# Attention logits made once, with queries on partitions, and weight halves transposed by DMA for the value product

## Chip, core and metric

One core of a Trainium2 chip runs the whole program in one launch. The metric is device time in microseconds; the kernel before took 2256.42 us (median of three runs, 2255.13 to 2261.94).

## What is computed

A decoder block with two parallel branches over 2048 tokens: sparse attention and a state-space recurrence, merged by gates. The change touches the attention branch. An indexer has chosen 256 keys for each query; in this kernel the choice is a mask `msk`, 0 for a chosen key and -2^60 for the others. The rest of the branch, cut from the reference (`k_sel` and `v_sel` are the chosen keys and values; a chosen key behind the query does not count):

```python
qg = qb.reshape(bsz, Q_BLOCK, ATTN_KV_HEADS, ATTN_GROUP, HEAD_DIM)   # 2 groups of 4 heads, 64 wide
s = jnp.einsum('btkgd,btskd->btkgs', qg, k_sel) * attn_scale
s = jnp.where(valid, s, -jnp.inf)
p = jax.nn.softmax(s, axis=-1)
o = jnp.einsum('btkgs,btskd->btkgd', p, v_sel)
o_a = o.reshape(bsz, Q_BLOCK, ATTN_WIDTH) * jax.nn.silu(z_a)
merged = g_a * (o_a @ w_branch_a) + g_b * (o_b @ w_branch_b)
x = x + merged @ w_out                                               # and a last RMSNorm
```

## The kernel before, in words

Every float32 operand of a large matmul is split in two float16 halves, high and low, and products are summed in PSUM from two or three matmuls of halves. The program runs in sections: normalised and transposed input, the state-space branch, the indexer, the selection beside the projections (until about 1410 us), then the attention and the merge, which is the place of the change.

Tokens are worked in 16 query tiles of 128; tile i has i+1 key tiles of 128. Keys stand transposed in `KK`, one high and one low part for each of the two groups (`KHt`, `K2t`), and the values in `Vt`, with a column of ones between high and low half. Three streams are written as Python generators, and `interleave` lays them beside each other at an even pace:

- `att_A(i)` (L1356) loads the queries of a tile, splits them, transposes both halves by DMA (`Q1`), and makes the largest masked logit of each query: one matmul `lq` of 512 columns (L1386) and one masked maximum on VectorE (L1389) for each head and 512 keys, queries on partitions. The negated maximum goes beside the queries into a second tile `q2t`, which another DMA transposes (`Q2`, L1404), so that the logits matmul subtracts it.
- `att_B(i)` (L1470) makes the logits a second time, now with keys on partitions and 4 heads x 128 queries as columns (L1483, L1485), adds the transposed mask `mkt` (L1492, loaded by a DMA transpose at L1353), takes the exponential (L1493), rounds it to float16 (`ph`, L1497) and subtracts for the low half (`pl`, L1500, GpSimd). Keys are already on the partitions, so `pv` (L1419) and `pv_lo` (L1428) use `ph` and `pl` as stationary sides as they are. `LAG` = 3 such steps lie between making a weight and using it. The column of ones gives the softmax sum. `tail` multiplies by the gate and splits and transposes the tile's output (`oT`).
- `fin_M` and `fin_O` (L1505 to L1577) are merge and output projection of earlier tiles: per tile 72 and 48 matmuls of 512 columns, with DMA loads `obt`, `gtl`, `xr` and a DMA transpose of the merged tile (`mT`). They fill PE between the attention's matmuls.

The generators give an emission order; the framework's scheduler then sets the order on each engine, and every DMA is issued from the one SP queue, in its order. Buffers come in rings (`bufs`), and an instruction waits until the ring's oldest user is done.

## Time and profile before

| | |
|---|---|
| runs | 2255.13, 2256.42, 2261.94 us |
| profiled execution | span 2252.5 us; no time of its own is listed, the median of the runs lies 3.9 us above the span |
| TensorE matmuls (PE) | 2045.4 us busy, 91% of the span |
| VectorE (DVE) | 1832.5 us, 81% |
| ScalarE (ACT) | 1129.4 us, 50% |
| GpSimd (POOL) | 840.0 us, 37% |
| DMA, one hardware queue | 226 MB, 37.8% of 16 engines |
| mean granted TensorE clock | 0.966 |

Busy time is the union of an engine's rows. A matmul's row lasts from its start to its modelled end and overlaps the next one, so a count of starts says more than busy time. "Granted clock" is the share of full speed that TensorE was given. An engine's idle time before an instruction is put down to the instruction or DMA that released it.

### The profile page before, as it was taken

The page shows a single profiled execution, that of the slowest core. Times are in us where ns is not written, and L with a number is a line of the kernel's source. Part 1 is how long each engine was busy: PE and PEld are TensorE (multiplying, and loading weights), DVE is VectorE, ACT ScalarE, POOL GpSimd, SP SyncE. Part 2 cuts the span into 40 slices and gives each one's busy share as a digit, 9 for nine tenths or more (in the row PEclk, how much of TensorE's full clock was granted, in tenths as well). Part 3 has the DMA queues.
Part 4 walks back from the last instruction along what each step waited for, and adds up shares of the span by engine and source line. Part 5 has one row for each costly group of instructions (what it writes and reads, how often), then busy time and mean ns, then how long its engine had stood idle before and what let it go on. Part 6 is the DMA issues. An engine that isn't in the chain of part 4 may idle for free. (4 is left out here: it accounts for less than half of the span.)

```text
span 2252.5 us, 43654 instructions
## 1 busy us (share of the span) xinstructions
PE 2045.4 (91%) x15537; PEld 1391.0 (62%) x15537; DVE 1832.5 (81%) x5156; ACT 1129.4 (50%) x1971; POOL 840.0 (37%) x1208
## 2 busy tenths in 40 slices
PE   6898998899998999899999987988988889999997
...
DVE  8888888988887588888988775577989888888864
...
GB/s 151 121 109 106 104 61 88 103 73 64 64 69 81 109 83 97 116 109 95 120 131 145 78 167 94 120 205 119 108 116 102 100 90 109 67 95 104 66 80 49
DMA packets 371196, 229.07 MB, mean 102 GB/s; under 512 B 209996, under 2 KB 333720, under 8 KB 370968
## 3 DMA queue, kind: packets, MB, share of 16 engines
q1 hardware_dynamic: 370968, 226.19, 37.8%
...
q14 instruction: 104, 0.85, 0.1%
...
## 5 line engine op out<-in xcount | busy, mean ns | idle before, releaser
L1500 POOL TENSOR_TENSOR pl<-p,ph 128x512 f16<-128x512 f32 x272 | 328.3, 1210 | 426.1 <-ACT ph L1497 407.5
L1493 ACT ACTIVATE p<-p,lnb,qsc 128x512 f32<-128x512 f32 x270 | 217.6, 811 | 213.0 <-DVE p L1492 212.8
L428 PEld LDWEIGHTS <-xh 128*128 128x128 f16 x2560 | 252.4, 100 | 46.6 <-ACT kvt L1178 10.3
L429 PEld LDWEIGHTS <-xh 128*128 128x128 f16 x2560 | 250.9, 99 | 47.4 <-issue 12.4
L430 PEld LDWEIGHTS <-xl 128*128 128x128 f16 x2560 | 250.9, 99 | 31.8 <-issue 1.9
L1492 DVE TENSOR_TENSOR p<-lg,mkt 128x512 f32<-128x512 f32 x266 | 181.5, 685 | 55.6 <-PE lg L1485 50.5
L1389 DVE CUSTOM_DVE_ANT_0 jk<-lq,mka 128x512 bf16<-128x512 f32 (+3 forms) x304 | 187.8, 618 | 24.8 <-PE lq L1386 18.7
L1497 ACT CAST ph<-p 128x512 f16<-128x512 f32 x272 | 165.8, 614 | 6.4
L1073 ACT ACTIVATE jkS<-sca,XX 128x384 int8<-128x384 f32 (+3 forms) x104 | 138.6, 1333 | 46.5 <-DVE XX L1063 30.3
L1419 PE MATMUL po<-Vt,ph 128*128 128x129 f16 x1088 | 114.6, 223 | 11.0 <-DVE oa L1442 4.1
L1386 PE MATMUL lq<-KK,Q 128*128 128x512 f16 (+3 forms) x320 | 102.6, 349 | 22.8 <-DVE mxs L1389 16.9
L1485 PE MATMUL lg<-Q,KK 128*128 128x512 f16 x272 | 103.7, 385 | 13.9 <-DMA Q<-q2t 13.9
L1075 DVE TENSOR_SCALAR_CACHE_REDUCE jkV<-sca,XX 128x1536 uint8<-128x1536 f32 (+4 forms) x78 | 111.8, 1434 | 2.4
L1562 PE MATMUL fi<-wo,mT 128*128 128x512 f16 x256 | 98.5, 385 | 10.9 <-DVE gtl L1538 5.1
L1483 PE MATMUL lg<-Q,KK 128*128 128x512 f16 x272 | 104.5, 385 | 2.8 <-DVE p L1492 2.8
L1531 PE MATMUL fi<-wpb,obt 128*128 128x512 f16 x256 | 99.2, 387 | 6.6 <-DVE gtl L1538 4.5
L937 ACT ACTIVATE r<-acc 128x512 f32<-128x512 f32 (+3 forms) x152 | 79.8, 541 | 46.4 <-DVE sca L938 28.8
L1428 PEld LDWEIGHTS <-pl 128*128 128x128 f16 x1088 | 66.3, 99 | 58.7 <-POOL pl L1500 6.1
L1419 PEld LDWEIGHTS <-ph 128*128 128x128 f16 x1088 | 72.3, 99 | 43.5 <-issue 10.8
L1532 PE MATMUL fi<-wpb,obt 128*128 128x512 f16 x256 | 99.0, 387 | 0.0
L1533 PE MATMUL fi<-wpb,obt 128*128 128x512 f16 x256 | 98.7, 386 | 0.0
L1563 PE MATMUL fi<-wo,mT 128*128 128x512 f16 x256 | 98.7, 386 | 0.0
(811 smaller groups left out, 6469.9 us busy)
## 6 DMA issues: line engine op xcount, KB each, us to landing
...
e<-ecr SPq DMA_DIRECT2D x128, 64.0 KB, 3.1
...
```

Source lines behind the costliest of these rows:

```text
L428: PE.matmul(ps, xh[:, c, tk], hi[:, c], start=(first and c == 0), stop=False)
L429: PE.matmul(ps, xh[:, c, tk], lo[:, c], start=False, stop=False)
L430: PE.matmul(ps, xl[:, c, tk], hi[:, c], start=False, stop=(last and c == KC - 1))
L1073: A.activation(jkA[:, :n], sct[i], AF.Sign, bias=thr[:, 0, k:k + 1], scale=-1.0, accum_out=cnt[:, 0, k:k + 1])
L1075: V.tensor_scalar(jkV[:, :n], sct[i], thr[:, 0, k:k + 1], 0.0, OP.is_lt, OP.add, accum_out=cnt[:, 0, k:k + 1])
L1389: V.tensor_tensor_reduce(jk[:, :c1 - c0], ps[:, :c1 - c0], mk[:, c0:c1], 1.0, -BIG, OP.add, OP.max, mxs_[:, h, c:c + 1])
L1419: PE.matmul(B["po"][h // 2][:, h % 2, 0:129], ph[:, h], Vt[:, j, g, 0:129], start=(j == 0 and h % 2 == 0), stop=False)
L1483: PE.matmul(ps, KHt[g][:, js], Q1[:, hs], start=True, stop=False)
L1492: V.tensor_tensor(p32, ps, mb, OP.add)
L1493: A.activation(p32, p32 if masked and not onP else ps, AF.Exp, bias=lnb, scale=qsc[g])
L1497: A.copy(ph, p32)
L1500: PL.tensor_tensor(pl, p32, ph, OP.subtract)
```

## The change

The logits are made once, with queries on partitions. `prep_q` loads and transposes a tile's queries. `weights_h` works one head: for each 512 keys two matmuls (high and low keys) and one masked-maximum instruction that also writes the masked logits to `xm`, carrying the running maximum from chunk to chunk; then one exponential over the whole row, with the maximum as its bias and the softmax sum as an accumulated output. In parts of up to `CH` = 1024 keys the weights are rounded to float16 (`hl`, first part), the remainder subtracted on GpSimd (second part), and both halves transposed by one DMA into `pT`. `values_h` multiplies `pT` by the values, the oldest head first, `LAG` = 2 heads after its weights. The separate maximum pass, `Q2`, the transposed mask and the column of ones are gone. The diff, cut to its core (the removed functions stand above; comments that it removes are left out):

```diff
@@ constants
-PLD = 2
-LAG = 3
-PB = 3
+LAG = 2
+CH = 1024
+XB = 3
+TB = 4
...
-PL_ = 2
-PQ_ = 2
+PL_ = 4
@@ class keys, tile
-            PL.memset(ks[:, :, :, 1, 66:128], 0.0)
-            PL.memset(ks[:, :, :, 1, 64:66], 2.0 ** 15)
...
-            V.tensor_tensor(ks[:, :, :, 1, 0:64], t[:, :, 0:2], ks[:, :, :, 0, 0:64], OP.subtract)
+            for hf in range(2):
+                V.tensor_tensor(ks[:, :, :, 1, hf * 64:hf * 64 + 64], t[:, :, 0:2], ks[:, :, :, 0, 0:64], OP.subtract)
@@ attention: att_A, att_B, pv, pv_lo and load_mt out
...
+    def load_mk(i):
+        mks[i] = at.tile([P, wide if wide < S else S], BF, name="mka")
+        SP.dma_start(mks[i][:, :(i + 1) * P], msk[i, :, :(i + 1) * P])
+    def prep_q(i):
+        q32 = at.tile([P, H, HD], FT, name="q32", bufs=1)
+        SP.dma_start(q32.rearrange("p h d -> p (h d)"), qd[i])
+        yield 1.0
+        while tails:
+            _run_all(tails.pop(0))
+        q1 = at.tile([P, H, 2, HD], F16, name="q1", tag="spa", bufs=1)
+        V.tensor_copy(q1[:, :, 0], q32)
+        V.tensor_tensor(q1[:, :, 1], q32, q1[:, :, 0], OP.subtract)
+        Qs[i] = ac.tile([P, H, P], F16, name="Q1", bufs=2)
+        SP.dma_start_transpose(Qs[i], q1.rearrange("p h a d -> p (h a d)"))
+        yield 2.0
+    def weights_h(i, h, B):
+        n = (i + 1) * P
+        g = h // 4
+        xm = pw.tile([P, wide], FT, name="xm", bufs=XB if wide == S else 2)
+        mxs_ = at.tile([P, 4], FT, name="mxs", bufs=4)
+        c = 0
+        for c0 in range(0, n, 512):
+            c, c1 = c0 // 512, min(n, c0 + 512)
+            ps = lgps2([P, 512])
+            PE.matmul(ps[:, :c1 - c0], Qs[i][:, h], KHt[g][:, c0:c1], start=True, stop=False)
+            PE.matmul(ps[:, :c1 - c0], Qs[i][:, h], K2t[g][:, c0:c1], start=False, stop=True)
+            mk = mks[i][:, c0:c1] if i >= 2 else cmask[:, 2 * P - n:]
+            V.tensor_tensor_reduce(xm[:, c0:c1], ps[:, :c1 - c0], mk, 1.0, mxs_[:, c - 1:c] if c else -BIG, OP.add, OP.max, mxs_[:, c:c + 1])
+            yield (c1 - c0) * 0.85e-3
+        yield None
+        nb = at.tile([P, 1], FT, name="nb", bufs=4)
+        V.tensor_scalar(nb, mxs_[:, c:c + 1], nqsc[g], LNB, OP.mult, OP.add)
+        A.activation(xm[:, :n], xm[:, :n], AF.Exp, bias=nb, scale=qsc[g], accum_out=B["den"][:, h:h + 1])
+        parts = []
+        for k0 in range(0, n, CH):
+            w = min(CH, n - k0)
+            hl = pw.tile([P, 2 * min(CH, wide)], F16, name="hl", bufs=2)
+            A.copy(hl[:, :w], xm[:, k0:k0 + w])
+            PL.tensor_tensor(hl[:, w:2 * w], xm[:, k0:k0 + w], hl[:, :w], OP.subtract)
+            pT = pw.tile([P, 2 * min(CH, wide) // P, P], F16, name="pT", bufs=TB)
+            SP.dma_start_transpose(pT[:, :2 * w // P], hl[:, :2 * w])
+            parts.append((k0 // P, w // P, pT))
+        pend.append((i, h, parts, B))
+    def values_h():
+        i, h, parts, B = pend.pop(0)
+        g, r = h // 4, h % 4
+        if r == 0:
+            B["po"] = psO.tile([P, 4, P], FT, name="po", tag="po")
+        po = B["po"]
+        for j0, nb_, pT in parts:
+            for b in range(nb_):
+                j = j0 + b
+                PE.matmul(po[:, r], pT[:, b], Vt[:, j, g], start=(r == 0 and j == 0), stop=False)
+                PE.matmul(po[:, r, 0:HD], pT[:, nb_ + b], Vt[:, j, g, 0:HD], start=False, stop=(r == 3 and j == i))
+                if b % 4 == 3 or b == nb_ - 1:
+                    yield (b % 4 + 1) * 0.086
+        if r == 3:
+            if g == 0:
+                while tails:
+                    _run_all(tails.pop(0))
+                B["oa"] = at.tile([P, H, HD], FT, name="oa", bufs=1)
+            rc = at.tile([P, 4], FT, name="rc")
+            oag = B["oa"][:, 4 * g:4 * g + 4]
+            V.reciprocal(rc, B["den"][:, 4 * g:4 * g + 4])
+            A.copy(oag, po[:, :, 0:HD])
+            V.tensor_tensor(oag, oag, po[:, :, HD:2 * HD], OP.add)
+            PL.tensor_tensor(oag, oag, rc[:, :, None].to_broadcast([P, 4, HD]), OP.mult)
+            if g == G - 1:
+                tails.append(tail(i, B))
...
+    def att(i):
+        B = {"den": at.tile([P, H], FT, name="den", bufs=2), "za": at.tile([P, H, HD], FT, name="za")}
+        SP.dma_start(B["za"].rearrange("p h d -> p (h d)"), zd[i])
+        n = i + 1
+        for h in range(H):
+            v = values_h() if len(pend) >= (LAG if wide == S else 1) else iter(())
+            ws = weights_h(i, h, B)
+            for w in _zip(iter(lambda: next(ws), None), v, (n + 3) // 4, (n + 3) // 4):
+                if tails and next(tails[0], True) is True:
+                    tails.pop(0)
+                yield w
+            for _ in ws:
+                pass
@@ fin_O
-        sq = fi.tile([P, 512], BF, name="sq", bufs=1)
+        sq = fi.tile([P, 512], I8, name="sq", bufs=1)
@@ pace
-    tA = lambda i: 2.0 + QY + 8 * (i + 1) * P / 2400
-    tB = lambda i: 2.0 * (i + 1)
+    tA = 3.0
+    tB = lambda i: 8 * (i + 1) * (0.85 * 0.128 + 0.086)
```

## The order around the change

Numbers behind a name count buffers. `lq`, `lg`/`lg2` and `fi2` are PSUM tiles, `jk` is scrap.

**DVE, query tile 6 (7 key tiles).** Before, the maxima of this tile (L1389, each with its accumulator read) stand between the masked copies `p32` of the tile before it (L1492):

```order
L1389 ISA jk_19881,mxs_19874<-lq_19879,mka_19749 128x384
L1389 ISA mxs_19874 128x1
L1492 TENSOR_TENSOR p32_19886<-lg2_19883,mkt_19304 128x512
L1389 ISA jk_19906,mxs_19874<-lq_19904,mka_19749 128x512
L1389 ISA mxs_19874 128x1
L1492 TENSOR_TENSOR p32_19919<-lg2_19916,mkt_19304 128x512
L1389 ISA jk_19910,mxs_19874<-lq_19908,mka_19749 128x384
L1389 ISA mxs_19874 128x1
```

Now L1369 writes the masked logits and their maximum at once, two instructions for each of a head's two chunks (512 and 384 keys), and `nb`, the bias of the exponential:

```order
L1374 TENSOR_SCALAR nb_20284<-mxs_20215,nqsc0_9090 128x1
L1369 ISA xm_20292,mxs_20293<-lg2_20294,mka_19707 128x512
L1369 ISA mxs_20293 128x1
L1517 TENSOR_SCALAR s1_19813<-s1_19813 128x1
L1421 TENSOR_TENSOR oa_20041<-oa_20041,za_19710 128x512
L1518 TENSOR_SCALAR s1_19813<-s1_19813 128x1
L1484 SCALAR_TENSOR_TENSOR gtl_20273<-gtl_20273,fi2_20275 128x512
L213 TENSOR_SCALAR fry_20251<-s1_19813 128x1
L1369 ISA xm_20292,mxs_20293<-lg2_20339,mka_19707,mxs_20293 128x384
L1369 ISA mxs_20293 128x1
L214 TENSOR_SCALAR fry_20251<-fry_20251 128x1
```

L1492 is gone from the queue, L1374 came, and the steps of the merge (`gtl`, `s1`, `fry`) stand between as before.

**SP, the DMA queue, at the same place.** Before, in a stretch with the mask loads of tile 7 (8 key tiles) and `Q2` of tile 6:

```order
L1336 DMA_TRANSPOSE mT_19949<-spm_19418 128x16x128
L1378 DMA_TRANSPOSE Q1_20361<-q1_20333 128x8x128
L1577 DMA out_x<-xr_19486 128x512
L1577 DMA out_x<-xr_19487 128x512
L1365 DMA mka_20240<-msk_9063 128x1024
L1353 DMA_TRANSPOSE mkt_20242<-msk_9063 128x8x128
L1554 DMA xr_20145<-in_x 128x512
L1404 DMA_TRANSPOSE Q2_20182<-q2t_9046 128x8x128
L1520 DMA gtl_20758<-gd_9096 128x2x512
L1554 DMA xr_20851<-in_x 128x512
L1361 DMA q32_22013<-qd_9094 128x512
```

Now, around the start of tile 6's heads; `pT` is a head's weights, 14 blocks of 128 columns:

```order
L1319 DMA_TRANSPOSE mT_20180<-spm_19761 128x16x128
L1383 DMA_TRANSPOSE pT_20212<-hl_20209 128x14x128
L1442 DMA za_20625<-zd_9084 128x512
L1383 DMA_TRANSPOSE pT_20290<-hl_20287 128x14x128
L1523 DMA out_x<-xr_19809 128x512
L1523 DMA out_x<-xr_19810 128x512
L1319 DMA_TRANSPOSE oT_20312<-spa_20299 128x8x128
L1383 DMA_TRANSPOSE pT_20359<-hl_20356 128x14x128
L1500 DMA xr_20368<-in_x 128x512
L1500 DMA xr_20904<-in_x 128x512
L1352 DMA_TRANSPOSE Q1_20322<-q1_20319 128x8x128
L1383 DMA_TRANSPOSE pT_20413<-hl_20410 128x14x128
```

The transposes of weights stand between the loads of the merge, and `Q2` and `mkt` are gone.

**PE, logits and value products.** Before, the logits of a step are followed by the value products of an earlier one:

```order
L1485 LDWEIGHTS KK_9097
L1485 MATMUL lg2_20865<-Q2_20658,KK_9097 128x512
L1419 LDWEIGHTS ph_20715
L1419 MATMUL po_20875<-Vt_9098,ph_20715 128x129
L1419 LDWEIGHTS ph_20715
L1419 MATMUL po_20875<-Vt_9098,ph_20715 128x129
L1531 LDWEIGHTS obt_20753
L1531 MATMUL fi2_20847<-wpb0_16607,obt_20753 128x512
```

Now, in tile 6, the last logits of the third head (chunk of 384 keys) and what follows them:

```order
L1366 MATMUL lg2_20339<-KK_9086,Q1_19874 128x384
L1367 LDWEIGHTS Q1_19874
L1367 MATMUL lg2_20339<-KK_9086,Q1_19874 128x384
L1477 LDWEIGHTS obt_20268
L1477 MATMUL fi2_20343<-wpb0_16597,obt_20268 128x512
L1478 LDWEIGHTS obt_20268
L1478 MATMUL fi2_20343<-wpb1_16598,obt_20268 128x512
L1479 LDWEIGHTS obt_20268
```

and the end of the stretch, up to its first value product (`pT_20359` holds its weights):

```order
L1508 LDWEIGHTS mT_20180
L1508 MATMUL fi2_20373<-wo0_18560,mT_20180 128x512
L1509 LDWEIGHTS mT_20180
L1509 MATMUL fi2_20373<-wo1_18561,mT_20180 128x512
L1510 LDWEIGHTS mT_20180
L1510 MATMUL fi2_20373<-wo0_18560,mT_20180 128x512
L1477 LDWEIGHTS obt_20268
L1477 MATMUL fi2_20343<-wpb0_16597,obt_20268 128x512
L1398 LDWEIGHTS pT_20359
L1398 MATMUL po_20324<-Vt_9087,pT_20359 128x128
```

Between the two stand 31 matmuls of merge and output, 8 of logits (the next two heads) and 14 pairs of value products (128 and 64 columns, the two heads before), 22,144 columns together. What was a distance of three steps of 512 columns is now one of one to five heads, which the scheduler set differently from tile to tile.

## Rows read from the trace of the kernel before

**Rows 1.** The page: busy us, share and instructions by engine; busy tenths of two engines.
```profile
PE 2045.4 (91%) x15537; PEld 1391.0 (62%) x15537; DVE 1832.5 (81%) x5156; ACT 1129.4 (50%) x1971; POOL 840.0 (37%) x1208
...
PE   6898998899998999899999987988988889999997
...
DVE  8888888988887588888988775577989888888864
```

**Rows 2.** Stretches of the attention part: length, busy us by engine, clock, DMA share, GB/s.
```profile
core 0: us, PE busy (x) PEld busy (x) DVE busy (x) ACT busy (x) POOL busy (x), PEclk, DMA share, GB/s
1470.00:1520.00 50.00, 41.17 (x231) 19.25 (x229) 37.85 (x113) 20.65 (x34) 14.99 (x16) 0.90 0.77 204
1520.00:1700.00 180.00, 158.64 (x1090) 80.93 (x1089) 155.66 (x465) 105.25 (x174) 82.55 (x81) 0.98 0.50 113
1700.00:1900.00 200.00, 182.50 (x1285) 94.36 (x1285) 176.43 (x490) 119.23 (x191) 92.07 (x87) 0.98 0.38 92
1900.00:2200.00 300.00, 280.87 (x2041) 148.59 (x2040) 247.16 (x634) 196.00 (x312) 151.45 (x137) 0.98 0.36 88
2200.00:2253.00 53.00, 38.81 (x191) 17.10 (x189) 21.02 (x68) 9.66 (x19) 0.80 (x2) 0.92 0.14 47
sum 783.00, PE 701.99 PEld 360.24 DVE 638.12 ACT 450.80 POOL 341.86; mean PE 140.40 PEld 72.05 DVE 127.62 ACT 90.16 POOL 68.37
```

**Rows 3.** Timeline of PE matmuls: start, row length, line, form, count.
```profile
1860.08 0.38 PE L1386 MATMUL lq<-KK,Q 128*128 128x512 f16 x1
1860.30 0.38 PE L1483 MATMUL lg<-Q,KK 128*128 128x512 f16 x1
1860.51 0.38 PE L1485 MATMUL lg<-Q,KK 128*128 128x512 f16 x1
1860.73 0.28 PE L1428 MATMUL po<-Vt,pl 128*128 128x65 f16 x4
1860.85 0.39 PE L1419 MATMUL po<-Vt,ph 128*128 128x129 f16 x4
1861.08 0.38 PE L1562 MATMUL fi<-wo,mT 128*128 128x512 f16 x1
```

**Rows 4.** Waits of PE, 1410 us to the end: total us, times, longest.
```profile
PE lq L1386 <- DVE mxs L1389: 16.9, 29, 1.7
PE lg L1485 <- DMA Q<-q2t: 13.9, 8, 3.2
PE fi L1562 <- DVE gtl L1538: 5.1, 3, 2.5
...
PE fi L1562 <- DMA mT<-spm: 4.6, 3, 2.2
PE fi L1531 <- DVE gtl L1538: 4.5, 3, 2.8
PE po L1419 <- DVE oa L1442: 4.1, 6, 1.4
...
PE lg L1483 <- DVE p L1492: 2.8, 3, 1.1
```

**Rows 5.** Groups by line, 1470 to 2200 us: count, busy us, mean ns, idle before.
```profile
L1500 POOL TENSOR_TENSOR pl<-p,ph 128x512 f16<-128x512 f32 x265 | 320.3, 1211 | 371.6 <-ACT ph L1497 367.6 <-DVE oa L1442 3.2 <-POOL pl L1500 0.2
L1493 ACT ACTIVATE p<-p,lnb,qsc 128x512 f32<-128x512 f32 x264 | 212.9, 811 | 210.9 <-DVE p L1492 210.7
L1492 DVE TENSOR_TENSOR p<-lg,mkt 128x512 f32<-128x512 f32 x263 | 179.5, 685 | 53.9 <-PE lg L1485 48.8 <-POOL pl L1500 3.1 <-PE po L1419 0.6
L1497 ACT CAST ph<-p 128x512 f16<-128x512 f32 x264 | 161.2, 614 | 6.3
L1389 DVE CUSTOM_DVE_ANT_0 jk<-lq,mka 128x512 bf16<-128x512 f32 x224 | 153.3, 684 | 20.4 <-PE lq L1386 16.0
...
L1389 DVE DVE_READ_ACCUMULATOR2_ANT mxs<- 128x1 f32 x296 | 24.2, 82 | 0.0
...
L1330 ACT ACTIVATE spm<-mg,rms 128x1024 f16<-128x1024 f32 x15 | 17.1, 1141 | 0.3 <-DVE rms L1323 0.2
...
L1330 ACT ACTIVATE spa<-oa,ras 128x512 f16<-128x512 f32 x13 | 9.3, 713 | 2.6 <-DVE ras L1323 2.5
...
L1541 ACT ACTIVATION_READ_ACCUMULATOR spm<-mg 128x1 f32 x29 | 5.4, 186 | 0.0
...
L1571 DVE TENSOR_SCALAR s<-s 128x1 f32<-128x1 f32 x14 | 2.9, 205 | 0.1
```

**Rows 6.** DMA transposes, 1470 us to the end: count, median us to landing.
```profile
mT<-spm SPq DMA_TRANSPOSE x15, 4.3
...
Q<-q2t SPq DMA_TRANSPOSE x13, 4.2
oT<-spa SPq DMA_TRANSPOSE x13, 3.1
```

**Rows 7.** Timeline of the SP queue: start, us that the issue takes.
```profile
1596.05 1.25 SPq L1353 DMA_TRANSPOSE mkt<-msk  x1
...
1598.02 1.73 SPq L1404 DMA_TRANSPOSE Q<-q2t  x1
```

More of the change, by code (lines that the diff above doesn't have):

```diff
@@ L874, in hybrid_block @@
     kv = pool("kv", 1, side="right", reuse_waits="tile")
-    lnb = kv.tile([P, 1], FT, name="lnb")
-    V.memset(lnb, 8 * math.log(2.0))
-    q2t = [kv.tile([P, H, P], F16, name="q2t")]
-    for t in q2t:
-        V.memset(t, 0.0)
     kctx = ExitStack()
@@ L1125, in hybrid_block @@
     KHt, K2t = ([KK[:, g, j] for g in range(G)] for j in range(2))
-    Vt = kv.tile([P, NT, G, 130], F16, name="Vt")
-    V.memset(Vt, 1.0)
+    Vt = kv.tile([P, NT, G, 2 * HD], F16, name="Vt")
     nsec = []
@@ L1225, in hybrid_block @@
     qsc = [cst.tile([P, 1], FT, name=f"qsc{k}") for k in range(2)]
+    nqsc = [cst.tile([P, 1], FT, name=f"nqsc{k}") for k in range(2)]
     kvs = keys()
@@ L1372, in att_A @@
         V.tensor_copy(q1[:, :, 0], q32)
         V.tensor_tensor(q1[:, :, 1], q32, q1[:, :, 0], OP.subtract)
-        A.copy(q2[:, :, 0:64], q1[:, :, 0])
-        yield 0.5
-        MARK("attA")
-        Q1 = ac.tile([P, H, P], F16, name="Q1", bufs=2)
-        SP.dma_start_transpose(Q1, q1.rearrange("p h a d -> p (h a d)"))
-        yield QY
-        mxs_ = at.tile([P, H, 4], FT, name="mxs")
-        for h in range(H):
-            for c in range(nck):
-                MARK("attA")
-                c0, c1 = c * 512, min(n, c * 512 + 512)
-                ps = psQ.tile([P, 512], FT, name="lq", tag="lq" if PQ_ else "lg2")
-                PE.matmul(ps[:, :c1 - c0], Q1[:, h], KHt[h // 4][:, c0:c1], start=True, stop=True)
-                jk = pw.tile([P, 512], BF, name="jk", tag="jk", bufs=1)
-                if i >= 2:
-                    V.tensor_tensor_reduce(jk[:, :c1 - c0], ps[:, :c1 - c0], mk[:, c0:c1], 1.0, -BIG, OP.add, OP.max, mxs_[:, h, c:c + 1])
-                else:
-                    if i == 1:
-                        V.tensor_reduce(mxs_[:, h, 1:2], ps[:, 0:P], axis=AX.X, op=OP.max)
-                    V.tensor_tensor_reduce(jk[:, :P], ps[:, n - P:n], cmask, 1.0, -BIG, OP.add, OP.max, mxs_[:, h, 0:1])
-                yield (c1 - c0) / 2400
@@ L1406, in att_A @@
-        yield 0.5
-    pend, plo, tails = [], [], []
-    def pv():
-        MARK("attB")
-        if len(plo) >= (PLD if lag > 1 else 1):
-            pv_lo()
-        i, g, j, ph, pl, B = pend.pop(0)
-        if j == 0:
-            B["po"] = [psO.tile([P, 2, 256], FT, name="po", tag="po") for _ in range(2)]
-        for h in range(4):
-            PE.matmul(B["po"][h // 2][:, h % 2, 0:129], ph[:, h], Vt[:, j, g, 0:129], start=(j == 0 and h % 2 == 0), stop=False)
-        plo.append((i, g, j, pl, B))
-        while j == i and plo:
-            pv_lo()
@@ L1464, in flush @@
         while pend:
[L1465 removed]
+            _run_all(values_h())
         while tails:
             _run_all(tails.pop(0))
[L1469 to L1503 removed]
@@ L1505, in att_B @@
                     tails.pop(0)
-                yield 1.0
+                yield w
+            for _ in ws:
+                pass
     def fin_M(i, fi):
```

139 lines of the change are left out of this document (29 added, 110 removed).

## The prediction, made before any run of the change

> **What bounds the kernel now.** I read the page first [rows 1]: TensorE (PE) is busy 91% of the span and VectorE (DVE) 81%, and both stay at eight or nine tenths in nearly every slice. The change lies in the attention part, so the table of stretches comes next [rows 2]. From 1470 us to the end PE is busy 702 of 783 us, DVE 638; ScalarE (ACT) 451 and GpSimd (POOL) 342 have room, and the DMA engines are at 0.36 to 0.50 after a start at 0.77. A busy matmul row overlaps the next one, so what PE must spend is read from the spacing of starts [rows 3]: matmuls of 512 columns start 0.215 us apart, 0.42 ns a column, four `ph` products of 129 columns take 0.23 us and four `pl` products of 65 take 0.12 us. From its first maximum matmul at 1410 us to the end PE has 1,920 matmuls of merge and output, 544 of logits and 272 of the maximum at 0.215 us, 1,088 pairs of value products at 0.0875, and 23 us of the last projection: 706 of 842 us. So PE is the bound, at 84%. Of the rest, 81 us from 1470 on are idle (the table's sum row), some 23 are half clock (a granted clock of 0.90 to 0.98), the others the latency of matmuls that something waits for. The waits of PE by name [rows 4] are small: 16.9 us for DVE's maxima, 13.9 us for the Q2 transpose, 5.1 and 4.5 us for DVE's merge, 4.1 us for `oa`.
>
> **What goes from PE.** The maximum pass `lq` (L1386) vanishes: for each key tile of each query tile 8 heads x 128 columns. Query tile i has i+1 key tiles, 136 in all, so 272 matmuls of 512 columns x 0.215 = **58 us**. The logits are still two matmuls per 512 columns (queries now the stationary side), and the value products are 128 + 64 columns where they were 129 + 65, so 0.70 us per key tile for 8 heads before and after.
>
> **What goes from DVE, ACT and POOL.** DVE loses the masked copy L1492, 263 x 0.685 = 180 us of its 638 [rows 5], the four small `rm` steps and half of the `oa` blocks, some 40 us; it gains one `nb` step per head, 112 x 0.2 = 22 us. It keeps the reduce with its accumulator read, 0.684 + 0.082 us per 512 columns; that instruction now also delivers what L1492 delivered. DVE falls to some 440 us. On ACT the exponential becomes one instruction per head. By the two lengths of L1330 [rows 5] 512 more columns cost 0.43 us, so a row of n key tiles costs 0.81 + 0.107 (n - 4), and 0.19 for its accumulator; 178 us over tiles 2 to 15 for 213. The copies to half precision cost about 150 for 161, the new `oa` copy 11. POOL's subtraction has the same elements, 1.21 us per 512. None of these three is the bound, before or after, so I count nothing for their totals. What frees PE is that a DVE at 60% keeps it waiting less: of the 33 us that it waits for DVE [rows 4] I take 20 as gone, and with Q2 its 13.9 go wholly: **34 us**. The edits in `keys` (no memsets, one more subtraction), the 8-bit `sq` and the wider `cmask` lie beside matmuls or on engines with room: nothing.
>
> **What comes on the DMA side.** Each head's weights, both halves, are transposed: 2 x 128 columns per key tile and head, 136 x 8 x 256 = 278,528 columns. No transpose of this source stands in the trace, but the same shape does: `mT` (2048 columns, SBUF to SBUF) lands 4.3 us after its issue starts, `oT` (1024) after 3.1 [rows 6], so 1024 columns cost 1.2 us over a fixed 1.9. That makes 326 us of all 16 engines; Q2 and `mkt` (33,000 columns) give back 39. The loop's own DMA time is its shares times its stretches, 320 us [rows 2]; it becomes about 600 of 770, a share near 0.78. The bytes: 1024 columns are 262 KB, in 1.2 us 218 GB/s. The Trainium skill (Advanced Engine Details and Errata, X-Bar Transpose (TRN2)) expects 350 to 400 GB/s; the trace is slower, no transpose in it comes near. By the page's figure the 326 us would be an estimated 190, and the share 0.6.
>
> On the SP queue 192 transposes come and 30 (16 Q2, 14 `mkt`) go. One holds the queue 1.25 to 1.73 us [rows 7], so some 240 us more of issue, in front of the loads of `gtl`, `xr`, `mT` and `oT`, which PE and DVE need. A transpose that waits for POOL also holds all that stands behind it. PE waits for `mT` today 4.6 us in three waits [rows 4]; with twice the DMA load I add 0.5 us for each of 16 tiles: **8 us**. Nothing bounds this from below; from above the Q2 transpose, 4.2 us against the 3.1 of an undisturbed one of its size [rows 6], gives 1.1 us, 18 us in all.
>
> **The new wait.** Before, a step of weights went DVE, ACT, ACT, POOL in 0.69 + 0.81 + 0.61 + 1.21 = 3.3 us and PE came back to it three steps later. Now a head's weights pass a chain after its last logits: reduce 0.77, `nb` 0.2, exponential, copy of up to 1024 columns (1.04), POOL (2.4), transpose (4.3 for 2048 columns), and some 0.5 us for the hand-offs. With the terms above that is 7.7, 8.7, 9.6 and 10.6 us for 5, 6, 7 and 8 key tiles, about 10.5 to 11.5 for more, and the second part of the weights of tiles with 9 and more key tiles lands up to 2.6 us later still. Against it stands PE's own work between a head's last logits and its first value product, counted as columns in the order of the changed program: 7.0, 7.0, 8.4 and 9.1 us on average for 5 to 8 key tiles (the head shown in the order part has 22,144 columns, 9.2 us), 13.7 for 9, 15 to 24 for 10 to 14, 10.1 for 15, and 13.6 for 16. To the chain I add 1 us of queue: undisturbed landings are at the median in `mT` and `oT`, and 1.1 us over it in Q2 [rows 6]. The gaps are then 1.7, 2.7, 2.2 and 2.5 us. Since a stall at one head also holds back the next head's logits, each gap is paid about half: 8 heads x half of 9.1 = 36 us. The last two tiles pay 12 us by their second parts, the first three 8 (their chain is 5 to 7 us, over 4 to 13 of work), and the end, where nothing is left to put between, about 6. Sum **62 us**. Bounds: 39 us with no queue at all, 116 with 3 us; each further us of chain costs about 27.
>
> **Clock.** In the stretch where PE was busy 41 of 50 us the granted clock was 0.90, elsewhere 0.98 [rows 2]. Tiles of 5 to 9 key tiles would now look like that stretch; 0.08 of 180 us is 14, half of it inside waits: **7 us**.
>
> **Sum.** -58 - 34 + 62 + 7 + 8 = -15 us. The profiled execution has a span of 2252.5 us; the median of the runs is 2256.4, 3.9 above it, which I leave as what lies around the span. So 2256 - 15 = **2241 us**, and for this case 2215 to 2262.
>
> **Rivals.**
> *The chain decides (slower).* If a head's weights take 3 us longer than the chain alone, by a blocked SP queue or a DMA queue with other transfers in it, the wait is 116 us instead of 62 and the time 2295; at 4 us 2325. For it: a DMA share near 0.78, in-order SP where `out_x` and `mT` wait for DVE, only two `hl` buffers, so that the copy of a part waits for the transpose two parts back. Against it: the undisturbed landings, and that tiles of 10 to 14 have twice the work between. It turns the sign at about 1.6 us of queue, where the sum is zero.
> *No new wait counts (faster).* PE's order holds enough work, and DVE's relief is real: -58 - 34 = 2164. For it: the slack of tiles 9 to 14; against it: tiles 5 to 8, where the chain is longer than the work even with no queue.
> *The DMA engines bound the loop.* The highest share of a stretch is 0.77. If 600 us cannot be done at more than that, the loop takes 779 of the 783 us it has now, and the time stays at 2252. For it: nothing in the trace runs higher; against it: that stretch was the start, with weights loading.
> That the change does not do what it says can be left out: the order no longer has L1386 or L1492.
>
> **Numbers.** A measurement of this kernel can tell about 0.3% (7 us) from no change. Forecast 0.45 (0.38 of it faster, 0.04 same, 0.03 slower); chain 0.30 (0.02 same, the rest slower); no new wait 0.17, faster; DMA bound 0.08 (0.04 same, 0.04 slower). Faster 0.55, same 0.10, slower 0.35. The range goes from 2165, the full gain, to 2325, the chain with 4 us of queue.
>
> **What would show it.** The new logits line of PE should have 0.215 us starts and no maximum matmuls; DVE near 60% in the loop; the weights' transposes landing at 4.3 to 5.5 us; DMA share about 0.75; PE waiting for `pT` some 60 us, most of it in tiles of 5 to 8 key tiles and hardly any at 10 to 14. Landings of 7 us, or waits for `pT` over 100 us or spread evenly over the tiles, would mean the chain; waits under 20 us the full gain. I am wrong in the mechanism if PE waits mainly for DVE, or if the granted clock falls below 0.9 over most of the loop.

## The result, and the profile after

| | before | after |
|---|---|---|
| median of the runs, us | 2255.99 (2255.13 to 2261.94, 4 runs) | 2340.53 (2334.59 to 2347.95, 4 runs) |
| ratio | | 1.0383, 95% interval 1.036 to 1.0407 |
| profiled execution's span, us | 2252.5 | 2339.4 |

The change is slower by 3.8%, 85 us, where the prediction had it faster by 15; it is also outside the range. The page of the changed kernel, against [rows 1], with the DMA engines' slices below PE's:

```profile
PE 2015.2 (86%) x15313; PEld 1363.9 (58%) x15313; DVE 1678.5 (72%) x4819; ACT 1074.3 (46%) x1891; POOL 807.6 (35%) x1079
...
PE   6799998899999899899998887788878777778877
...
DMA  4443423322223322423453444977886777888981
```

PE has 224 matmuls and 30 us of busy time less; the maximum pass is gone. But its last third stands at seven and eight tenths, where it stood at eight and nine. The stretches, with the columns of [rows 2]:

```profile
1470.00:1520.00 50.00, 35.99 (x177) 16.11 (x176) 23.80 (x73) 19.41 (x46) 12.69 (x13) 0.80 0.98 238
1520.00:1700.00 180.00, 146.47 (x984) 72.15 (x982) 113.48 (x358) 87.42 (x159) 62.68 (x42) 0.97 0.80 170
1700.00:1900.00 200.00, 155.93 (x1065) 77.62 (x1063) 108.07 (x332) 88.93 (x147) 69.19 (x52) 0.97 0.73 156
1900.00:2200.00 300.00, 236.64 (x1728) 120.05 (x1727) 183.83 (x508) 145.69 (x199) 133.70 (x78) 0.96 0.83 171
2200.00:2340.00 140.00, 101.64 (x685) 49.53 (x683) 68.63 (x202) 52.03 (x71) 35.94 (x20) 0.94 0.58 120
sum 870.00, PE 676.67 PEld 335.47 DVE 497.81 ACT 393.49 POOL 314.20; mean PE 135.33 PEld 67.09 DVE 99.56 ACT 78.70 POOL 62.84
```

From 1470 us on PE is now busy 677 of 870 us (702 of 783 before), DVE 498: DVE has room, and PE is less busy all the same. The DMA share is 0.73 to 0.83 from 1520 to 2200 us, where it was 0.36 to 0.50. What PE waits for, and who waits for the weights' chain, from 1410 us to the end (total us, times, longest), against [rows 4]:

```profile
PE po L1398 <- DMA pT<-hl: 118.5, 100, 3.7
PE lg L1366 <- DVE mxs L1369: 48.2, 33, 2.4
PE fi L1508 <- DMA mT<-spm: 4.6, 3, 2.5
...
POOL hl L1381 <- ACT hl L1380: 498.1, 122, 18.6
ACT hl L1380 <- DMA pT<-hl: 120.4, 69, 6.1
DVE xm L1369 <- POOL hl L1381: 96.0, 46, 5.6
```

PE waits 118.5 us for `pT` and 48.2 for DVE's maxima, though DVE is at 57%. The lines below say why DVE is late: DVE itself waits 96.0 us for POOL to let go of an `xm` buffer, and ACT's copy waits 120.4 us for the transposition to let go of an `hl` buffer. The steps of the chain cost what they were taken for ([rows 5] for those of before):

```profile
L1381 POOL TENSOR_TENSOR hl<-xm,hl 128x1024 f16<-128x1024 f32 x64 | 138.5, 2164 | 297.6 <-ACT hl L1380 297.6
L1369 DVE CUSTOM_DVE_ANT_0 xm<-lg,mka,mxs 128x512 f32<-128x512 f32 x98 | 73.4, 749 | 43.9 <-PE lg L1367 40.3 <-DVE frt L216 0.4
L1369 DVE CUSTOM_DVE_ANT_0 xm<-lg,mka 128x512 f32<-128x512 f32 x97 | 66.8, 688 | 101.4 <-POOL hl L1381 78.9 <-PE lg L1367 21.7 <-issue 0.3
L1380 ACT CAST hl<-xm 128x1024 f16<-128x1024 f32 x64 | 66.5, 1039 | 83.3 <-DMA pT<-hl 79.2 <-POOL oa L1413 3.3
L1374 DVE TENSOR_SCALAR nb<-mxs,nqsc 128x1 f32<-128x1 f32 x104 | 21.6, 210 | 1.6
```

The copy of 1024 weights takes 1.04 us and POOL's subtraction 2.16; the transpositions of the weights land 4.3 us after their issue starts (median of all sizes, 1470 to 2200 us; 4.4 for those of 2048 columns), where `mT` took 4.3 in [rows 6]. One turn of a buffer can be read in the timeline, where PE is at the third head of the tile with 12 key tiles and the parts, 1024 and 384 keys, are those of the last two heads of the tile before (start, us, engine, line; x2 is two instructions in a row; in brackets the wait before it and what ended it):

```profile
1907.97 1.03 ACT L1380 CAST hl<-xm 128x1024 f16<-128x1024 f32 x1
...
1909.13 3.00 POOL L1381 TENSOR_TENSOR hl<-xm,hl 128x1024 f16<-128x1024 f32 x2 [5.49 <-ACT hl L1380]
1909.56 0.51 ACT L1380 CAST hl<-xm 128x384 f16<-128x384 f32 x1 [0.56 <-DMA pT<-hl]
...
1911.28 3.70 SPq L1383 DMA_TRANSPOSE pT<-hl  x2
...
1912.16 0.69 DVE L1369 CUSTOM_DVE_ANT_0 xm<-lg,mka 128x512 f32<-128x512 f32 x1 [4.29 <-POOL hl L1381]
...
1912.91 0.38 PE L1366 MATMUL lg<-KK,Q 128*128 128x512 f16 x1 [0.74 <-DVE mxs L1369]
...
1915.72 1.04 ACT L1380 CAST hl<-xm 128x1024 f16<-128x1024 f32 x1 [3.99 <-DMA pT<-hl]
```

At 1907.97 ACT copies a part of 1024, POOL subtracts from 1909.13 (two parts in this row), SP issues from 1911.28, and only at 1915.72, after 3.99 us of waiting for that transposition, can ACT make the next copy of 1024: 7.75 us for one turn. Meanwhile DVE waits 4.29 us for POOL at 1912.16, and PE 0.74 us for DVE. A head of 9 or more key tiles has two parts, and there are two buffers: one turn for each head, 7.75 us here, where PE's own work of that tile is 47.7 / 8 = 6.0 us a head. In the tiles of 10 to 14 key tiles the copies of a head's first part start 7.7 us apart at the least and 8.5 on average. The four `pT` buffers don't hold the chain up: SP's own waits before these transpositions name POOL alone and never PE, which frees `pT` (1410 us to the end).

```profile
SPq L1383 <- POOL hl L1381: 247.0, 90, 6.1
SPq L1383 <- POOL oa L1413: 51.3, 18, 6.5
```

Counted from the starts and columns of the trace, with three of the experiments below beside it:

```
key tiles              10     11     12     13     14     15   9 to 15
us from a tile's first logits to the next tile's
  after              61.0   66.5   72.3   72.2   78.4   80.9   480
  three hl (e2)      55.0   61.1   63.5   66.4   74.1   79.7   452
  parts of 512 (e4)  53.5   56.2   57.4   65.6   75.4   72.8   432
  one hl (e9)        92.2   94.0  103.5  121.7  113.0  116.2   725
us from the end of a head's exponential to the end of its last copy, mean
  after              17.6   18.7   16.9   16.5   11.8    3.6
  three hl (e2)       3.0    3.2    2.5    2.5    2.1    2.4
  parts of 512 (e4)   3.1    2.3    2.2    3.1    2.5    3.5
```

The 56 heads of 9 to 15 key tiles take 8.6 us each in the changed kernel, the turn and a little. PE's own work between those starts, its columns at 0.417 ns, is 331 us for 9 to 15 in each of the first three rows.

### The profile page after: what moved, and what is told of

Read it like the earlier page. It is cut to its first block, busy times and chain, and to the rows that moved or that the text cites. A ratio compares the mean times of both kernels' runs of the same rounds, so it can differ in the third digit from the quotient of the medians.

```text
span 2339.4 us, 42576 instructions
## 1 busy us (share of the span) xinstructions
PE 2015.2 (86%) x15313; PEld 1363.9 (58%) x15313; DVE 1678.5 (72%) x4819; ACT 1074.3 (46%) x1891; POOL 807.6 (35%) x1079
## 5 line engine op out<-in xcount | busy, mean ns | idle before, releaser
L1381 POOL TENSOR_TENSOR hl<-xm,hl 128x1024 f16<-128x1024 f32 (+7 forms) x192 | 306.5, 1609 | 519.0 <-ACT hl L1380 498.1
L1375 ACT ACTIVATE xm<-xm,nb,qsc 128x128 f32<-128x128 f32 (+15 forms) x128 | 165.1, 1290 | 198.7 <-DVE nb L1374 188.5
L1398 PE MATMUL po<-Vt,pT 128*128 128x128 f16 x1088 | 127.5, 225 | 119.9 <-DMA pT<-hl 118.5
L1380 ACT CAST hl<-xm 128x1024 f16<-128x1024 f32 (+7 forms) x192 | 149.0, 792 | 129.0 <-DMA pT<-hl 120.4
L1398 PEld LDWEIGHTS <-pT 128*128 128x128 f16 x1088 | 98.2, 100 | 187.9 <-DMA pT<-hl 175.5
L1369 DVE CUSTOM_DVE_ANT_0 xm<-lg,mka,mxs 128x512 f32<-128x512 f32 (+3 forms) x192 | 124.4, 648 | 80.5 <-PE lg L1367 74.1
L1366 PE MATMUL lg<-KK,Q 128*128 128x512 f16 (+3 forms) x320 | 117.2, 370 | 57.9 <-DVE mxs L1369 48.2
L1369 DVE CUSTOM_DVE_ANT_0 xm<-lg,mka 128x512 f32<-128x512 f32 (+1 forms) x112 | 76.0, 678 | 116.0 <-POOL hl L1381 88.1
L1399 PE MATMUL po<-Vt,pT 128*128 128x64 f16 x1088 | 120.5, 196 | 0.0
L1367 PE MATMUL lg<-KK,Q 128*128 128x512 f16 (+3 forms) x320 | 118.1, 372 | 0.0
L1399 PEld LDWEIGHTS <-pT 128*128 128x128 f16 x1088 | 97.9, 100 | 10.6 <-issue 1.7
L1477 PE MATMUL fi<-wpb,obt 128*128 128x512 f16 x256 | 100.9, 394 | 3.0 <-DMA obt<-obn 1.7
L1478 PE MATMUL fi<-wpb,obt 128*128 128x512 f16 x256 | 100.8, 394 | 0.0
L1479 PE MATMUL fi<-wpb,obt 128*128 128x512 f16 x256 | 100.3, 392 | 0.0
```

The lines of the kernel that those rows point to most:

```text
L1366: PE.matmul(ps[:, :c1 - c0], Qs[i][:, h], KHt[g][:, c0:c1], start=True, stop=False)
L1367: PE.matmul(ps[:, :c1 - c0], Qs[i][:, h], K2t[g][:, c0:c1], start=False, stop=True)
L1369: V.tensor_tensor_reduce(xm[:, c0:c1], ps[:, :c1 - c0], mk, 1.0, mxs_[:, c - 1:c] if c else -BIG, OP.add, OP.max, mxs_[:, c:c + 1])
L1375: A.activation(xm[:, :n], xm[:, :n], AF.Exp, bias=nb, scale=qsc[g], accum_out=B["den"][:, h:h + 1])
L1380: A.copy(hl[:, :w], xm[:, k0:k0 + w])
L1381: PL.tensor_tensor(hl[:, w:2 * w], xm[:, k0:k0 + w], hl[:, :w], OP.subtract)
```

## The experiments

Theory 1 was the ring: two `hl` buffers, each held through copy, subtraction and transposition, set the pace of the tiles with two parts a head. Theory 2 was the DMA engines, whose share had risen to what the prediction's third rival feared. Others came up on the way. All have the runs of the kernel before on the same chips beside them (medians 2253.8 to 2254.6 us).

**Control (e1).** To make room for buffers, `fin_M` and `fin_O` lose one each.

```diff
-            gt = fi.tile([P, 2, 512], FT, name="gtl")
+            gt = fi.tile([P, 2, 512], FT, name="gtl", bufs=1)
-        xr = [fi.tile([P, 512], FT, name="xr", bufs=3) for _ in range(2)]
+        xr = [fi.tile([P, 512], FT, name="xr", bufs=2) for _ in range(2)]
```

> Control: the changed kernel with one buffer fewer for each of two tiles of merge and output (gtl 2 to 1, xr 3 to 2), which only frees 6 KB of each partition for the next two kernels. Both theories: a load of gtl or xr can no longer run ahead, so the same 2340 us or up to 15 us more (2335 to 2355).

Measured: 2343.4 us, ratio 1.0405 (1.0374 to 1.0435). The room is as good as free here.

**A third buffer (e2).** The control, and:

```diff
-            hl = pw.tile([P, 2 * min(CH, wide)], F16, name="hl", bufs=2)
+            hl = pw.tile([P, 2 * min(CH, wide)], F16, name="hl", bufs=3)
```

> The control with three hl buffers for two. Theory 1, the ring: a buffer is held by copy 1.04 + subtraction 2.16 + transposition 4.3 us, about 7.5 to 8, and with two parts for a head from 9 key tiles on, two buffers allow one head in 8 us; three allow one in 5.3, less than PE's work from 10 key tiles on (5.3 to 7.6 us). Then the waits of the copy for a transposition (120 us) fall below 40, and of the 105 us that PE idles in tiles of 10 to 16 key tiles about half goes: 2285 to 2305 us. Theory 2, DMA capacity: the transpositions take the time they need of the 16 engines, another buffer only lengthens their queue: landings grow from 4.3 us to 6 or more, time within 10 us of the control.

Measured: 2305.0 us, ratio 1.0247 (1.0214 to 1.0280), 38 us under the control. Waits of this kernel, as above:

```profile
PE po L1398 <- DMA pT<-hl: 131.5, 97, 7.8
...
ACT hl L1380 <- DMA pT<-hl: 42.6, 31, 4.2
...
DVE xm L1369 <- POOL hl L1381: 20.5, 13, 4.4
...
PE lg L1366 <- DVE mxs L1369: 8.5, 9, 1.7
```

The copy's wait falls from 120.4 to 42.6 us, PE's wait for DVE from 48.2 to 8.5, and the landings stay at a median of 4.3 us. Theory 2 wanted landings of 6 us and no gain. So it is the ring of `hl`. The three `xm` buffers are a link of the chain and not its cause: their number is the same here, and DVE's wait for one falls from 96.0 to 20.5 us. PE's wait for `pT` itself stays, at 131.5. PE's order changes with the buffer too, since the scheduler sets it anew: in tiles of 10 to 13 the value products stand 2.0 to 2.2 heads behind their logits, where they stood 3.9 to 4.9. A fourth `hl` buffer of this size has no room beside the others (their pool would need 56 KB of each partition, where 54 are left), so four were not measured.

**One buffer (e9).** The changed kernel, with the dose the other way.

```diff
-            hl = pw.tile([P, 2 * min(CH, wide)], F16, name="hl", bufs=2)
+            hl = pw.tile([P, 2 * min(CH, wide)], F16, name="hl", bufs=1)
```

> The changed kernel (parts of 1024, 2340 us) with one hl buffer for two: the dose the other way. The ring: every part of 1024 keys takes copy 1.04 + subtraction 2.16 + issue and transposition 4.3 and about 0.7 of hand-offs, 8 us, one after the other, and the short part of a head 4 to 8. Tiles of 9 to 16 key tiles need 12 to 16 us a head, 8 x 8 x 14 = 900 us where the changed kernel takes 530; tiles of 5 to 8 need 6 to 8 us a head, 225 for 172. So 2340 + 370 + 50 = 2760 us, 2680 to 2860. DMA capacity or the SP queue as the cause of the loss: the transpositions are the same and the engines were the limit already, so less than 100 us more.

Measured: 2745.9 us (one run). Waits from 1410 us to the end, and the stretch from 1900 to 2200 us:

```profile
ACT hl L1380 <- DMA pT<-hl: 580.8, 169, 9.7
DVE xm L1369 <- POOL hl L1381: 463.3, 105, 11.7
PE po L1398 <- DMA pT<-hl: 379.9, 151, 8.6
```

```profile
1900.00:2200.00 300.00, 170.38 (x1022) 81.77 (x1022) 103.56 (x317) 92.41 (x140) 77.32 (x55) 0.75 0.49 105
```

The 56 heads of 9 to 15 key tiles take 725 us, 13 us each. The DMA share falls to 0.49 while PE's waits for `pT` treble: the engines aren't full, the chain is long. Three doses, 2746, 2340 and 2305 us, go the way of theory 1.

**Smaller parts in the same bytes (e4).**

```diff
-CH = 1024
+CH = 512
-TB = 4
+TB = 8
-            hl = pw.tile([P, 2 * min(CH, wide)], F16, name="hl", bufs=2)
+            hl = pw.tile([P, 2 * min(CH, wide)], F16, name="hl", bufs=4)
```

> The changed kernel with parts of 512 keys instead of 1024, and four hl and eight pT buffers of half the size, so the same bytes in the ring. Theory 1, the ring: copy 0.6 + subtraction 1.25 + transposition 3.1 us is about 5.2 us for a buffer, four buffers allow a part of 512 every 1.3 us, 3 parts (9 to 12 key tiles) in 4 us, 4 parts in 5.2; also the latency of a head's last part falls by some 2.5 us in all tiles: 2250 to 2280 us. Theory 2, DMA capacity: 1024 columns cost the engines at least as much as half of 2048, and there are about 320 transpositions for 176: unchanged or slower, 2335 to 2380. A third possibility, the SP queue: 140 more issues of 1.2 us or more hold it 170 us longer; loads of merge and output come late, and the gain is under 30 us.

Measured: 2278.2 us, ratio 1.0111 (1.0082 to 1.0141): 62 us back without a byte more. Waits and three stretches:

```profile
PE po L1398 <- DMA pT<-hl: 106.2, 90, 4.4
ACT hl L1380 <- DMA pT<-hl: 46.0, 57, 4.1
...
PE lg L1366 <- DVE mxs L1369: 2.5, 7, 0.6
```

```profile
1470.00:1520.00 50.00, 38.57 (x205) 17.82 (x204) 27.01 (x81) 23.96 (x56) 15.66 (x16) 0.86 1.09 239
...
1700.00:1900.00 200.00, 163.62 (x1201) 83.82 (x1200) 129.03 (x396) 110.65 (x200) 94.30 (x93) 0.97 0.89 181
1900.00:2200.00 300.00, 257.66 (x1921) 133.46 (x1920) 182.38 (x542) 170.51 (x278) 153.67 (x148) 0.94 0.94 183
```

PE's waits for DVE are gone (2.5 us). The 128 further transpositions on SP (320 for 192) don't outweigh it. The DMA share is now 0.94, and 1.09 in the stretch at the start, so a share is no share of a capacity that ends at 1. The next run asks what it means.

**Half the columns (e5).** Parts of 512, and only the low halves transposed:

```diff
-            SP.dma_start_transpose(pT[:, :2 * w // P], hl[:, :2 * w])
+            SP.dma_start_transpose(pT[:, :w // P], hl[:, w:2 * w])
-                PE.matmul(po[:, r, 0:HD], pT[:, nb_ + b], Vt[:, j, g, 0:HD], start=False, stop=(r == 3 and j == i))
+                PE.matmul(po[:, r, 0:HD], pT[:, b], Vt[:, j, g, 0:HD], start=False, stop=(r == 3 and j == i))
```

> The kernel with parts of 512 (2278 us) with only the low halves transposed: the value product's high matmul takes the low half's block in place of the high one's, so every matmul, copy and subtraction is still there and the transposition still waits for POOL, but it moves 512 columns for 1024. What is left out of the result is the high half of the weights. DMA capacity, if it is what still holds this kernel (share 0.85 to 0.99 in tiles of 7 to 16 key tiles): 139,000 columns at 1.2 us for 1024 are 163 us of the engines, the share falls to about 0.7, and the time by 40 to 70 us, 2210 to 2240. Latency: the landing falls from 3.3 to about 2.6 us, 0.7 us x 27 for each us of chain is 19: 2255 to 2265. SP queue: still 320 issues of 1.2 us, so at most 10 us less.

Measured: 2269.2 us (2261.3 to 2279.9, 6 runs), ratio 1.0073 (1.0043 to 1.0103), 9 us less. The stretch that stood at 0.94, and PE's wait:

```profile
1900.00:2200.00 300.00, 255.79 (x1966) 135.36 (x1965) 185.49 (x547) 168.94 (x279) 154.86 (x147) 0.97 0.60 127
```

```profile
PE po L1398 <- DMA pT<-hl: 111.7, 87, 4.9
```

The share falls from 0.94 to 0.60 and landings from 3.3 to 2.5 us, yet PE waits as long for `pT` (111.7 for 106.2). Theory 2 falls here too: at a share of 0.94 the engines were not what held the loop.

**Three heads behind (e6).** Parts of 512, and more of PE's work between a head's logits and its value product. The edit names tiles of up to 8 key tiles:

```diff
-            v = values_h() if len(pend) >= (LAG if wide == S else 1) else iter(())
+            v = values_h() if len(pend) >= ((3 if i < 8 else LAG) if wide == S else 1) else iter(())
```

> The kernel with parts of 512 (2278 us), and the value product of a head three heads behind its logits instead of two in tiles of 3 to 8 key tiles (for more the eight pT buffers do not hold three heads). Latency: PE gets one more head's work, 3.6 to 5 us, between logits and value product, and the waits for pT in those tiles (some 6 to 7 us of idle PE in each) nearly go: 25 to 35 us less, 2243 to 2253. DMA capacity or SP queue: the same transpositions in the same time, under 8 us less.

Measured: 2264.9 us, ratio 1.0045 (1.0028 to 1.0062), 13 us less where 25 to 35 were expected. PE's two largest waits, and a stretch:

```profile
PE fi L1508 <- DMA mT<-spm: 41.4, 10, 6.9
PE po L1398 <- DMA pT<-hl: 41.1, 39, 4.9
```

```profile
1700.00:1900.00 200.00, 170.06 (x1255) 90.42 (x1254) 130.09 (x406) 116.63 (x206) 104.85 (x101) 0.92 0.97 193
```

The edit does more than it names. `att` takes one head off the list for each that it adds, so the third head stays on the list after tile 8: in the trace the first value product stands 3.0 heads behind in all tiles of 5 to 15 key tiles, where the kernel with parts of 512 has 2.0 to 2.2. The eight `pT` buffers bear it, SP waits 1.8 us for PE before these transpositions. The wait for `pT` falls by 65 us, 17 of them in tiles of 5 to 8 and 38 in those of 9 to 14, as latency has it. A wait of 41.4 us for the merged tile's transposition, which the kernels above had at 11.3 us at most (1.7 with parts of 512), takes 40 us of that back. The granted clock, 0.92 from 1700 to 1900 us where it was 0.97, takes some of the rest.

**The same with half the columns (e10)** (e6 with the edit of e5):

> The kernel with parts of 512 and the value product three heads behind in tiles of 3 to 8 key tiles (2265 us), with only the low halves transposed and used twice (the high half of the weights is left out of the result). There the DMA share stood at 0.9 to 1.04 in tiles of 7 to 16 and PE waited 41 us for mT and 41 for pT. DMA capacity as the new limit: both waits fall by more than half, 2200 to 2230. Latency as what is left: 2250 to 2260, as 9 us was all that half the columns gave at two heads behind.

Measured: 2248.0 us, ratio 0.9970 (0.9955 to 0.9985), 17 us under e6: nearer to the latency's figure. Of the two waits 38.0 us for `pT` and 33.0 for `mT` are left with the columns halved. So most of the wait for `mT` isn't DMA load either. That the transposition stands too close behind its merge is what the next run tries.

**The merged tile transposed on PE (e11).** e6, and in `fin_M`:

```diff
-        yield from split_T(mg, s_m, t, mT, KC, i == NT - 1)
+        yield from split_T(mg, s_m, t, mT, KC, True)
```

> The kernel with parts of 512 and three heads behind in tiles of 3 to 8 (2265 us), with the merged tile (mT) of every tile transposed on PE, as the last tile's already is, instead of by DMA. PE gets 15 x 16 transpositions of 128 columns, some 0.06 us each, 15 us; 41 us of waits for mT go, and 15 DMA transpositions of 2048 columns with them (some 36 us of the engines). Where mT's wait was a symptom of the full DMA queue the whole gain stays: 2235 to 2250. Where the wait passes on to pT: 2260 to 2275.

Measured: 2244.7 us (2241.7 to 2246.8, 5 runs), ratio 0.9963 (0.9949 to 0.9977). This beats both kernels, the one before by 10 us. What PE waits for most:

```profile
PE po L1398 <- DMA pT<-hl: 42.5, 33, 4.3
...
PE lg L1326 <- ACT spm L1313: 27.6, 12, 7.5
```

Without the DMA, PE waits 27.6 us for ACT's rounding of the merged tile (`spm`): the transposition does stand too close behind it, whoever makes it.

**More of it (e12).** e11, the diff of the control, and:

```diff
-TB = 8
+TB = 11
-        yield from split_T(oaf, s_a, t, oT, 4, i == NT - 1)
+        yield from split_T(oaf, s_a, t, oT, 4, True)
-            v = values_h() if len(pend) >= ((3 if i < 8 else LAG) if wide == S else 1) else iter(())
+            v = values_h() if len(pend) >= ((3 if i < 12 else LAG) if wide == S else 1) else iter(())
```

> As the run before (mT on PE), and oT on PE as well (15 x 8 transpositions, 7 us of PE), eleven pT buffers for eight (room from one gtl and one xr buffer fewer, which cost 0 to 8 us alone), and three heads behind up to 12 key tiles. Latency: the waits for pT in tiles of 9 to 12 (7 to 10 us of idle PE in each) fall by half, 2225 to 2245, below the kernel before. DMA capacity: tiles of 11 and 12 stand at a share of 1.0, so no gain over the run before, 2240 to 2265.

Measured: 2283.5 us, ratio 1.0137 (1.0120 to 1.0154), a miss. Three waits:

```profile
DVE gtl L1484 <- DMA gtl<-gd: 68.0, 14, 8.2
...
PE fi L1477 <- DVE gtl L1484: 55.9, 12, 7.4
...
PE po L1398 <- DMA pT<-hl: 27.4, 28, 3.4
```

The wait for `pT` did shrink, from 42.5 to 27.4 us, but not by the third head: e11 has it in these tiles already (2.9 to 3.0 heads behind up to 15 key tiles in both traces), so the last line of the edit changes no distance. DVE now waits 68.0 us for the load of the single `gtl` buffer (7.2 in e11 with two, 11.6 in the control with one), and PE 55.9 for DVE. What the other edits are worth alone wasn't tried.

**The merged tile's transposition later (e13).** e11, and in `split_T`, ahead of the transposition on PE:

```diff
         yield SPY
+        for _ in range(3 if pe and nb == KC else 0):
+            yield SPY
         if not pe:
```

> The kernel with parts of 512, three heads behind in tiles of 3 to 8, and mT transposed on PE (2245 us), with three more steps of other streams written between the rounding of the merged tile and its transposition on PE. There PE waited 33 us for that tile (27.6 us for ScalarE's copy, 5.3 for DVE's low half), because the transposition stood 4 to 7 us of PE work behind the merge. Now it stands 6 to 10 us behind in most tiles, 3 to 5 in some. Latency in PE's order as what is left: 10 to 25 us less, 2220 to 2235. If what PE gains there it loses to the waits for pT or the DMA queue: 2238 to 2250.

Measured: 2285.9 us, ratio 1.0139 (1.0122 to 1.0157), 41 us slower, a miss. The wait for ACT's copy fell from 27.6 to 5.0 us, but each `yield SPY` also counts as 2 us of work in the pacing of the merge stream (`_pace`). That stream fell behind: after the start of the last logits came 149 us with 169 triples of merge matmuls, where e11 has 74 us with 68. Work that should fill PE beside the attention ran alone behind it.

**Loads on ScalarE's queue (e7).** Parts of 512, with `gtl`, `xr`, `out`, `za`, the mask and the queries issued from ACT; one of the six lines:

```diff
-                SP.dma_start(out[rows, cs_], xr[nh])
+                A.dma_start(out[rows, cs_], xr[nh])
...
```

> The kernel with parts of 512 (2278 us), and the plain loads and stores of the loop (gtl, xr, out, za, the mask and the queries) issued from ScalarE's queue instead of SP's. SP's issues of the loop are 581 us, 417 of them transpositions of weights; 59 us of issue, and the waits of the stores for DVE (48 us), leave SP. SP queue as what holds the transpositions (they start 1.3 to 2.8 us after POOL is done): that shrinks by about 1 us, 20 to 27 us less, 2250 to 2258. Latency or capacity: within 8 us, or up to 15 slower where ScalarE is held up by a store that waits for DVE.

Measured: 2323.7 us, ratio 1.0314 (1.0279 to 1.0349), 46 us slower than without.

```profile
PE po L1398 <- DMA pT<-hl: 142.8, 101, 5.8
...
ACT hl L1380 <- DVE xr L1522: 14.9, 7, 4.4
```

ACT's copies stood 14.9 us behind stores that waited for DVE, and PE's wait for `pT` grew by 37 us. SP's queue, freed of these issues, gave little: in tiles of 5 to 14 key tiles a head's last transposition was issued 0.1 to 0.4 us sooner after POOL's subtraction, where 1 us was expected, and those of 1024 columns landed in 4.1 us on average where they took 3.7. Why they landed later stays open.

**Subtraction on DVE (e8).** Parts of 512, and:

```diff
-            PL.tensor_tensor(hl[:, w:2 * w], xm[:, k0:k0 + w], hl[:, :w], OP.subtract)
+            V.tensor_tensor(hl[:, w:2 * w], xm[:, k0:k0 + w], hl[:, :w], OP.subtract)
```

> The kernel with parts of 512 (2278 us), with the subtraction for the low half on DVE instead of POOL. DVE gets 320 instructions of about 0.65 us, 190 us on top of 508, and stands at some 80% of the loop; POOL's 1.25 us leaves the chain and DVE's 0.65 enters. Latency: 0.6 us less chain, 16 us less, 2258 to 2266, if DVE's in-order queue does not delay the maxima; if it does (DVE then is the bound or the subtraction stands behind reduces of later heads), 2285 to 2320. DMA capacity: within 8 us.

Measured: 2296.3 us, ratio 1.0183 (1.0148 to 1.0218), 18 us slower.

```profile
ACT xm L1375 <- DVE nb L1374: 208.9, 81, 12.3
PE po L1398 <- DMA pT<-hl: 122.8, 108, 5.6
```

The exponential waits 38 us longer for DVE's `nb` (170.6 before), which stands behind subtractions, and `pT` comes later, not earlier. POOL's slower subtraction beside DVE is the better place.

## Why the prediction was wrong, by its own steps

**The step that failed** is the new wait, +62 us, and in it the sentence "15 to 24 for 10 to 14" with its reading that these tiles hardly wait. It set the chain of one head against PE's work in front of that head, as a latency, and took the `hl` buffers to be free whenever a head came. A second question wasn't priced: how often the two buffers come round. The numbers for it stood in the prediction: 1.04 + 2.4 + 4.3 is 7.7 us for a turn, and two parts in two buffers give one head a turn. PE's work a head is 5.3, 5.7, 6.0, 5.8 and 6.8 us in tiles of 10 to 14, so each of them had to wait, 8 x (7.75 - work) = 15 us on average. In these tiles the work in front of a head grows with the delay, and does not help: copies ended 12 to 19 us after the exponential. The two `hl` buffers were named among the arguments of the rival *the chain decides*, but priced there as 3 or 4 us more of latency.

The sum of the waits shows the size. Forecast were 62 us for `pT` and the 13 that were left of the old waits for DVE, 75; measured are 118.5 + 48.2 = 167. The 92 us between are most of the 99 by which the time was missed. Counted from the traces, by the tile whose head waits (us; the forecast's first three tiles stand under 1 to 4, its end under 15 and 16):

```
key tiles                           1 to 4   5 to 8   9 to 14   15, 16    all
forecast, for pT                         8       36         0       18     62
after, for pT                           15       31        47       25    118
after, for DVE's maxima                  3        0        42        2     48
three hl (e2), for pT                   12       29        64       26    131
parts of 512 (e4), for pT               14       23        49       20    106
three heads behind (e6), for pT         13        6        11       11     41
```

The tiles of 5 to 8, where the latency was worked out, came near the forecast, 31 for 36. Some 89 of the 92 us lie in tiles of 9 to 14, which were put at nothing. The ring accounts for DVE's part, which is gone in e2 and e4, but not for all of `pT`'s. The "15 to 24" us of work were the ring's own mark: in the changed kernel the value products of 10 to 13 key tiles stand 3.9 to 4.9 heads behind their logits. With three buffers or with parts of 512 they stand two heads behind, as `LAG` asks, over 9.0 and 8.1 us of work (mean of 9 to 14), and PE waits 64 and 49 us for `pT` there. So these tiles had little slack with or without the ring. The kernel with parts of 512, which takes 62 us back, the ring's and some latency of a head's last part, stands at 2278. Of its 106 us of waits for `pT` most are latency: three heads behind, with 13.4 us of work in front in tiles of 9 to 14, 41 are left.

**Right:** the steps of the chain (copy, POOL, landing of 4.3 us), DVE at 57% for "near 60%", a DMA share of 0.73 to 0.83 for 0.75 to 0.78, and the 58 us of PE's maximum pass, gone by the count of matmuls. **Its own test** held as well: waits for `pT` over 100 us "or spread evenly over the tiles, would mean the chain": they are 118.5 us, 31 for the heads of 5 to 8 key tiles and 32 for those of 10 to 14, with 42 for DVE on top in the second. PE waiting mainly for DVE, the sign against the mechanism, came in the tiles of 10 to 14 alone. **Wrong in size:** the 8 us more for `mT` didn't come (4.6 us before and after). Of the 34 us from old waits Q2's went, but PE waited 48.2 us for DVE, not 13, since DVE was held by POOL through the ring. The clock's term was 7 us; the stretches give 1 minus the granted clock times their length, 42 us from 1470 us on for 23 before ([rows 2]), so some 19, part of it inside waits. **DMA engines bound the loop:** the share came, the bound didn't (e2, e5).

The price of a column nearly held: by their own sizes 2048 columns land in 4.4 us (median), 1024 in 3.4 (e4), 512 in 2.5 (e5). The second 1024 columns, 262 KB, cost 1.1 us, some 240 GB/s, and the 512 before them 0.9 us, some 150. The Trainium skill (DMA: Bandwidth & Descriptors, Latency and other measured facts) gives 261 GB/s for a transposing DMA whose middle dimension isn't contiguous and 350 to 400 for a contiguous one. These runs stay under both, though each block of `pT` is written whole.
